# Folding three key blocks into two in a neighbourhood-attention kernel, with a reordered projection piece and exchanged PSUM pools

## The chip, the core and the metric

The kernel runs on one core of a Trainium2 chip. The metric is the device time of one execution in microseconds (us); smaller is better. The engines are named as the profile names them: PE is TensorE's matmul, PEld its weight load, DVE is VectorE, ACT is ScalarE, POOL is GpSimd, and SP is SyncE, which issues most of the DMAs. Each has an instruction queue of its own that runs in order; the engines wait for one another by semaphores.

## The reference

A two-layer encoder trunk on 1024 tokens (a grid of 16 rows by 64 columns) of width 1024, all in float32. Cut to what is computed:

```python
for i in range(2):
    h = rms_norm(x, norm_g[i])
    y = mixer_a(h, ...) if i == 0 else mixer_b(h, ...)
    x = x + y                                  # y already holds the output projection
    g = sigmoid(rms_norm(x, ple_norm_g[i]) @ ple_w_gate[i])
    x = x + g * (p[i] @ ple_w_proj[i])
return rms_norm(x, final_norm_g)

def mixer_a(h):   # 16 heads of 64
    q, k, v, gate = split(h @ w_in, 4)
    # each query sees 8 rows x 16 columns of keys, clamped at the grid's edge, plus a bias by 2-D offset
    o = softmax(q . k[window] / 8 + rpb) @ v[window]
    return (o * silu(gate)) @ w_out

def mixer_b(h):   # 16 query heads, 4 key heads, rms-normalised and rotated q and k, all 1024 keys
    o = softmax(q . k / 8) @ v
    return (o * silu(gate)) @ w_out
```

## The kernel before

**Numbers.** Every float32 operand of a projection is held as a rounded high part and a low remainder, and a product is three matmuls: high by high, high by low, low by high (`split3`). Tile names end in h and l for the two parts (`HTh`/`HTl` the normalised stream, transposed; `wh`/`wl` a weight; `PTh`/`PTl` the transposed softmax numerators).

**Stages.** Mixer A's prologue (norm, first V projection); mixer A's 16 heads; the output projection, gate and norm of layer 0 (`dense_phase(0)`); mixer B's prologue; mixer B; `dense_phase(1)`. The program's order is written out by hand, engine by engine, as the Python code runs; nothing is rescheduled.

**Mixer A.** Tokens are laid out so that a tile of 128 is all 16 rows of an 8-column strip, and there are 8 tiles j. The 16-column window of a query in tile j reaches from its own column in tile j-1 to the column just below it in tile j+1, so an inner tile (j = 1 to 6) needs three key tiles, and an edge tile two. The mask `MK` blocks, in the left tile, columns under the query's and, in the right one, columns at or over it: of each pair of columns in the left and the right tile exactly one is valid. A step is one (head, tile). Its parts:

- `f_S`: two matmuls make the scores `s` of 128 queries against 384 keys (256 at an edge); DVE adds the bias table `tb` and takes the row minimum in one instruction (L741).
- `f_E`: ACT takes the exponential (L750).
- `f_T`: PE transposes each block of 128 into `t` (L758), ACT copies it as `PTh` (L761), DVE writes the remainder `PTl` (L762).
- `f_AV`: two matmuls per key tile, `PTh` and `PTl` by V, add up the output `o`. It runs for the step two back.

`head_end` scales and gates a finished half head. Its two products on POOL, Y by the gate G (L563) and Y by the reciprocal row sums `rb` (L564), are put into the program four steps after the half's last AV, and `rb` comes by two DMAs over DRAM. POOL also makes the bias table (L716, five products a head, at tile 1) and issues the accumulating DMAs that add up weight blocks (L632).

**mix.** In each head a list `att` of these parts is interleaved with a list `dense` of projection pieces (the next head's q and k, the gate, the last embedding product), by weights (`CA` in A, `CB` and `CN` in B): after a part, pieces follow while their share lags. Each part also ticks `post`, a list of callbacks with a delay in parts; `QD` holds the delays of a head's q and k splits. A piece's last matmul calls `leave`, which copies its PSUM bank out. `hold` pieces are kept for the end.

**Mixer B.** A step is one query tile of a head against all 1024 keys: scores in two PSUM banks (`psS`), minimum on DVE (L1198), exponential on ACT (L1204), then eight transposes in two groups of four (L1214), each group copied by ACT (`PTh`, L1216) and DVE (`PTl`, L1217) out of one of two banks `psT`. Two steps share one AV of 16 matmuls, which follows the odd step. `q_stack` (L1168) transposes a new query block into `psT`, once in eight steps. Only one bank `d` serves the projection pieces.

**PSUM.** Eight banks. Pools take banks in the order in which they are opened. `dense_phase` opens `ps_t` (four banks for transposes) and then `ps_d` (four for products); mixer A had opened d, s, t, o with two banks each; mixer B opens d (bank 0), s (1 to 4), t (5 and 6), o (7). Where a stage starts, a bank is free once the last reader of the stage before is through.

## Time and profile before

| | |
|---|---|
| three runs, median (lowest to highest) | 1531.45 us (1528.62 to 1531.79) |
| the profiled execution's own time | 1530.75 us |
| its span, first to last instruction | 1528.9 us (1.85 us lie around it) |
| prologue of A, 0 to 60 us | DVE busy 38.06, ACT 36.11, POOL 15.71 us |
| dense phase of layer 0, 531 to 711 us | PE busy 177.12, DVE 145.11, ACT 79.73 us |
| prologue of B, 711 to 765 us | PE busy 52.94, DVE 43.42 us |
| dense phase of layer 1, 1345 to 1529 us | PE busy 174.08, DVE 139.65 us |

The rows of the two mixers are with the prediction. A row of a view with groups reads: line, engine, operation, output<-inputs, shapes, count | busy us, mean ns of one | idle time of that engine just before them and what ended it. A row of the timeline reads: start, length, engine, line, what, count of merged instructions, and in brackets the engine's idle time before it with its releaser. Matmuls are pipelined, so the length of one overlaps the next; the distance between two starts tells what one costs.

### The profile page before, as it was taken

The page shows a single profiled execution, that of the slowest core. Times are in us where ns is not written, and L with a number is a line of the kernel's source. Part 1 is how long each engine was busy: PE and PEld are TensorE (multiplying, and loading weights), DVE is VectorE, ACT ScalarE, POOL GpSimd, SP SyncE. Part 2 cuts the span into 40 slices and gives each one's busy share as a digit, 9 for nine tenths or more (in the row PEclk, how much of TensorE's full clock was granted, in tenths as well). Part 3 has the DMA queues.
Part 4 walks back from the last instruction along what each step waited for, and adds up shares of the span by engine and source line. Part 5 has one row for each costly group of instructions (what it writes and reads, how often), then busy time and mean ns, then how long its engine had stood idle before and what let it go on. Part 6 is the DMA issues. An engine that isn't in the chain of part 4 may idle for free.

```text
span 1528.9 us, 24361 instructions
## 1 busy us (share of the span) xinstructions
PE 1499.4 (98%) x8976; PEld 1314.0 (86%) x8976; DVE 1102.1 (72%) x2091; ACT 899.4 (59%) x1801; POOL 304.4 (20%) x413
## 2 busy tenths in 40 slices
PE   8999999999999999999999999999999999999997
PEld 8888988988988888888988889989899888878786
DVE  7566576477477599767887786777877877789856
ACT  6565465466366635433467676676767777745432
POOL 1222232142112000010222132453141300000022
PEclk9999999999999999999999999999999999999999
DMA  8325355272122962262210111111101122763123
GB/s 256 119 95 140 83 142 162 63 165 85 36 87 66 334 247 97 90 201 79 77 49 21 32 39 50 46 32 43 58 27 47 37 77 70 234 225 115 67 88 134
DMA packets 91096, 157.22 MB, mean 103 GB/s; under 512 B 18144, under 2 KB 54112, under 8 KB 90464
## 3 DMA queue, kind: packets, MB, share of 16 engines
q1 hardware_dynamic: 85824, 139.66, 27.9%
q0 software_dynamic: 2560, 8.39, 3.2%
q10 hardware_dynamic: 2592, 7.61, 1.4%
q8 instruction: 71, 1.16, 0.3%
q14 instruction: 49, 0.40, 0.1%
HBM read 125.10 MB, written 50.83 MB: 115 GB/s over the span
## 4 chain that ended last, share of the span: by engine, by line
PE 80%; DVE 11%; ACT 5%; issue 2%; DMA 1%; SPq 0%; ACTq 0%; DVEq 0%
PE d L317 50%; PE o L317 10%; PE s L317 8%; PE t L1214 6%; PE t L758 3%; DVE PTl L1217 2%; PE t L317 1%; PE t L467 1%; DVE mn L1198 1%; DVE xn L1541 1%; ACT PTh L1216 1%; ACT P L1204 1%; ACT wh L226 1%; DVE X L1437 1%; DVE HTl L1383 1%
## 5 line engine op out<-in xcount | busy, mean ns | idle before, releaser
L317 PE MATMUL d<-wh,HTh 128*128 128x256 f32 (+1 forms) x1032 | 343.3, 335 | 6.0 <-DVE HTl L469 2.3
L317 PE MATMUL d<-wh,HTl 128*128 128x256 f32 (+1 forms) x1032 | 338.3, 330 | 0.3 <-DVE HTl L469 0.3
L317 PE MATMUL d<-wl,HTh 128*128 128x256 f32 (+1 forms) x1032 | 337.0, 328 | 0.0
L1217 DVE TENSOR_TENSOR PTl<-t,PTh 128x512 fp32r<-128x512 f32 x256 | 164.4, 683 | 111.4 <-ACT PTh L1216 111.1
L317 PEld LDWEIGHTS d<-wh,HTh 128*128 128x128 f32 x1032 | 195.1, 190 | 25.8 <-DVE HTl L469 2.5
L317 PEld LDWEIGHTS d<-wl,HTh 128*128 128x128 f32 x1032 | 194.9, 190 | 19.0
L317 PEld LDWEIGHTS d<-wh,HTl 128*128 128x128 f32 x1032 | 195.1, 190 | 18.7 <-DVE HTl L469 0.5
L317 PE MATMUL d<-HTh,wh 128*128 128x512 f32 x504 | 206.0, 409 | 0.0
L317 PE MATMUL d<-HTh,wl 128*128 128x512 f32 x504 | 198.3, 394 | 0.0
L317 PE MATMUL d<-HTl,wh 128*128 128x512 f32 x504 | 197.6, 392 | 0.0
L1204 ACT ACTIVATE P<-s,mn 128x1024 f32<-128x1024 f32 x128 | 142.8, 1116 | 67.5 <-DVE mn L1198 66.7
L1216 ACT ACTIVATE PTh<-t 128x512 fp32r<-128x512 f32 x256 | 139.7, 593 | 45.1 <-PE t L1214 44.6
L1198 DVE TENSOR_REDUCE mn<-s 128x1 f32<-128x1024 f32 x128 | 154.7, 1209 | 12.3 <-PE s L317 12.3
L1214 PE MATMUL t<-ident,P 128*128 128x128 f32 x1024 | 137.2, 275 | 4.8 <-DVE PTl L1217 1.7
L317 PE MATMUL s<-KA,QS 128*128 128x512 f32 (+2 forms) x384 | 133.7, 402 | 0.0
L1214 PEld LDWEIGHTS t<-ident,P 128*128 128x128 f32 x1024 | 114.7, 140 | 20.1 <-DVE PTl L1217 12.6
L231 DVE TENSOR_TENSOR wl<-wstage,wh 128x1024 fp32r<-128x1024 f32 x78 | 101.7, 1308 | 34.7 <-ACT wh L226 34.2
L317 PE MATMUL s<-KB,QS 128*128 128x512 f32 (+2 forms) x384 | 121.8, 371 | 0.0
L317 PE MATMUL o<-PTh,V 128*128 128x256 f32 (+2 forms) x672 | 118.9, 288 | 1.2 <-DVE Y L483 0.9
L317 PE MATMUL o<-PTl,V 128*128 128x256 f32 (+2 forms) x672 | 119.1, 288 | 0.1
L762 DVE TENSOR_TENSOR PTl<-t,PTh 128x384 fp32r<-128x384 f32 (+1 forms) x128 | 66.6, 520 | 71.3 <-ACT PTh L761 70.1
L317 PEld LDWEIGHTS d<-HTh,wl 128*128 128x128 f32 x504 | 94.7, 188 | 21.6
(237 smaller groups left out, 2700.9 us busy)
## 6 DMA issues: line engine op xcount, KB each, us to landing
wstage<-in_wts SPq DMA_DIRECT2D x88, 512.0 KB
pp<-ppD SPq DMA_DIRECT2D x32, 256.0 KB
X<-in_x SPq DMA_DIRECT2D x15, 512.0 KB
rb<-rD SPq DMA_DIRECT2D x56, 128.0 KB
ppD<-th SPq DMA_DIRECT2D x20, 256.0 KB
tD0t<-in_wts SPq DMA_DIRECT2D x16, 256.0 KB
tD1t<-in_wts SPq DMA_DIRECT2D x16, 256.0 KB
xD<-X SPq DMA_DIRECT2D x8, 512.0 KB
```

The costliest lines, as they stand in the source:

```text
L226: act.activation(hi, s, AF.Copy)
L231: eng.tensor_tensor(lo[:, c:c + n], s[:, c:c + n], hi[:, c:c + n], ALU.subtract)
L317: pe.matmul(ps, a, b, start=first, stop=last, skip_group_check=True)
L467: pe.transpose(ps[:, k], xn[:, (4 * c + k) * 128:(4 * c + k + 1) * 128], ident)
L758: pe.transpose(ps[:, i], sp[:, i * 128:(i + 1) * 128], ident)
L762: dve.tensor_tensor(PTl[:, sl], ps[:, :m], PTh[:, sl], ALU.subtract)
L1198: dve.tensor_reduce(mn, ps, axis=AX.X, op=ALU.min)
L1204: act.activation(p, ps, AF.Exp, bias=mn, scale=-1.0, accum_out=RS[h, hf][:, t:t + 1])
L1214: pe.transpose(ps[:, i], p[:, k * 128:(k + 1) * 128], ident)
L1216: act.activation(PTh[:, ks, c], ps, AF.Copy)
L1217: dve.tensor_tensor(PTl[:, ks, c], ps, PTh[:, ks, c], ALU.subtract)
L1383: dve.tensor_tensor(al(t + m, c), src[m], ah(t + m, c), ALU.subtract)
```

## The change

1. **Folding in mixer A.** For an inner tile, DVE now copies, in PSUM, the right tile's scores over the left tile's wherever the mask `SIDE[:, 2]` (key column under the query's) says so, by `copy_predicated` (128 queries by 128 keys). The left table block gets the right one's entries in the same way, once a head (`join`). Minimum, exponential, transposes and the two copies of the transposed blocks then run on 256 columns, where they ran on 384. POOL takes the folded transposed block apart again: one product by `SIDE[:, :2]` for `PTh` and one for `PTl`, each 128 by 256, into the two places that AV reads. The folded block lies in one of two new slots of `PTh` and `PTl`.
2. AV runs for the step three back, so `head_end` and its POOL products come a step later.
3. The copies of a head's k into the other 64 partitions (`KA`, `KB`) go from DVE to ACT, with five callbacks (`QD` of five) where there were three. A DMA of 192 KB loads `SIDE` in the prologue.
4. **Mixer B.** `mix` puts a projection piece ahead of an odd step's transposes where none has stood since the even step's; `q_stack` waits for the next piece (`after`); three pieces are held for the end where there were two, and the last odd step may take one of them.
5. `dense_phase` opens `ps_d` before `ps_t`: products in banks 0 to 3, transposes in 4 to 7.

```diff
-QD = (2, 5, 8)
+QD = (2, 4, 6, 7, 9)
+    sides = np.stack([c[:, None] >= c[None, :], c[:, None] < c[None, :], c[:, None] > c[None, :]], axis=1).astype(np.float32)
@@ mix
+        since = True
         for i, (f, c) in enumerate(att):
+            kind = getattr(f, "kind", None)
+            if kind == "apart" and not since and (dense or len(kept) > 2):
+                d, e = (dense or kept).pop(0)
+                d()
+                spent += e
+                after.run()
+            if kind in ("apart", "blocks"):
+                since = False
             f()
...
                 spent += c
+                since = True
+                after.run()
@@ qk_evac
-                    def two():
+                    def low_q():
                         dve.scalar_tensor_tensor(qs[hi, s], raw[lo], -0.125, qs[lo, s], op0=ALU.mult, op1=ALU.subtract)
+                    def low_k():
                         dve.tensor_tensor(kb[hi, s], raw[hi], ka[hi, s], ALU.subtract)
-                        dve.tensor_copy(ka[lo, s], ka[hi, s])
-                    def three():
-                        dve.tensor_copy(kb[lo, s], kb[hi, s])
+                    def across(k):
+                        act.activation(k[lo, s], k[hi, s], AF.Copy)
+                    parts = (one, low_q, lambda: across(ka), low_k, lambda: across(kb))
@@
+            def join(h):
+                dve.copy_predicated(TB[h][:, 1], SIDE[:, 2].bitcast(mybir.dt.int32), TB[h][:, 3])
@@ f_S
-                    tb = TB[h][:, 1:4]
-                sp = sb.tile([128, 384], F32, name="sp", bufs=3)
+                    tb = TB[h][:, 1:3]
+                    dve.copy_predicated(ps[:, 0:128], SIDE[:, 2].bitcast(mybir.dt.int32), ps[:, 256:384])
+                sp = sb.tile([128, 256], F32, name="sp", bufs=3)
@@ f_T
-                for i in range(m):
-                    pe.transpose(ps[:, i], sp[:, i * 128:(i + 1) * 128], ident)
+                for i in range(2):
+                    c = 1 - i if inner else i
+                    pe.transpose(ps[:, i], sp[:, c * 128:(c + 1) * 128], ident)
...
+                if inner:
+                    def apart():
+                        for pt in (PTh, PTl):
+                            pool.tensor_tensor(pt[:, 3 * j - 1:3 * j + 4:4], pt[:, f1:f1 + 1].to_broadcast([128, 2, 128]), SIDE[:, :2],
+                                               ALU.mult)
+                    apart()
@@ mixer_a
-                    if n >= 2:
-                        att += av_and_v(*steps[n - 2])
+                    if n >= 3:
+                        att += av_and_v(*steps[n - 3])
@@ mixer_b
-                        att.append((lambda hn=hn, fn=fn: q_stack(hn // 2, fn), 0.0))
+                        att.append((lambda hn=hn, fn=fn: after(lambda: q_stack(hn // 2, fn)), 0.0))
...
-                mix(att, dense, hold=HOLD if g == 3 else 0)
+                mix(att, dense, hold=HOLD + 1 if g == 3 else 0)
@@ dense_phase
+            ps_d = es.enter_context(tc.tile_pool(name="dps", bufs=4, space=PSUM))
             ps_t = es.enter_context(tc.tile_pool(name="dpt", bufs=4, space=PSUM))
-            ps_d = es.enter_context(tc.tile_pool(name="dps", bufs=4, space=PSUM))
```

Three places show how the instructions move. The first is PE in mixer A, at two inner steps of one head: t are the transposes, s the scores, d a projection piece of six matmuls (its first row stands for it), o the AV. Before:

```order
L758 MATMUL t<-ident,sp 128x128 [waits Activation_49]
L758 MATMUL t<-ident,sp 128x128 x2
L317 MATMUL s<-KA,QS 128x384 [waits PE_49]
L317 MATMUL s<-KB,QS 128x384
L317 MATMUL d<-HTh,wh_2073 128x512
...
L317 MATMUL o<-PTh,V 128x384
L317 MATMUL o<-PTl,V 128x384 [waits DVE_49]
```

With the change:

```order
L779 MATMUL t<-ident,sp 128x128 [waits PE_49,Activation_49]
L779 MATMUL t<-ident,sp 128x128
L318 MATMUL s<-KA,QS 128x384 [waits PE_49]
L318 MATMUL s<-KB,QS 128x384
L318 MATMUL d<-HTh,wh_2170 128x512
...
L318 MATMUL o<-PTh,V 128x384 [waits Pool_49]
L318 MATMUL o<-PTl,V 128x384 [waits Pool_49]
```

One transpose of three is gone, the scores stay as they were, and AV now waits for POOL. POOL's own queue over the same stretch of a head gets two products (L789) for every inner step, among the table and the products of `head_end`:

```order
L733 TENSOR_TENSOR tb<-MK,u 128x128 [waits DMAHW6_49]
L733 TENSOR_TENSOR tb<-MK,u 128x128 x4
L789 TENSOR_TENSOR PTh<-PTh,SIDE 128x2x128 [waits Activation_49]
L789 TENSOR_TENSOR PTl<-PTl,SIDE 128x2x128 [waits DVE_49]
...
L577 TENSOR_TENSOR Y<-Y,G 128x512
L578 TENSOR_TENSOR Y<-Y,rb 128x512 [waits DMAHW1_49,DMAHW0_49,Pool_49]
```

The products that wait for the DMA of `rb` stand ahead of later L789 products in the same queue.

The second place is PE at the first two steps of mixer B. Before, the odd step's eight transposes follow the even step's scores directly, and the piece d comes after them:

```order
L1214 MATMUL t<-ident,P 128x128 x8
L317 MATMUL s<-KA,QS 128x512 x2
L317 MATMUL s<-KB,QS 128x512 x2
L1214 MATMUL t<-ident,P 128x128 x8
L317 MATMUL d<-wh_8110,HTh 128x256
```

With the change:

```order
L318 MATMUL s<-KA,QS 128x512 x2
L318 MATMUL s<-KB,QS 128x512 x2
L318 MATMUL d<-wh_8320,HTh 128x256
...
L1247 MATMUL t<-ident,P 128x128 x8
L318 MATMUL s<-KA,QS 128x512 x2
L318 MATMUL s<-KB,QS 128x512 x2
L318 MATMUL o<-PTh,V 128x256 x8
```

The piece has gone ahead of the transposes, and AV (o) now follows the odd step's scores with no piece between.

The third place is PE at the first projection of mixer B's prologue, into bank 0, which follows the last transposes of the dense phase. Before and after:

```order
L467 MATMUL t<-ident,xn 128x128 [waits PE_49,Activation_49]
L467 MATMUL t<-ident,xn 128x128 x3
L317 MATMUL d<-wh_6865,HTh 128x256 [waits DVE_49]
L317 MATMUL d<-wl_6866,HTh 128x256
L317 MATMUL d<-wh_6865,HTl 128x256
```

```order
L481 MATMUL t<-ident,xn 128x128 x3
L318 MATMUL d<-wh_7075,HTh 128x256 [waits Activation_49]
L318 MATMUL d<-wl_7076,HTh 128x256
L318 MATMUL d<-wh_7075,HTl 128x256
```

The wait for DVE, which reads transposes out of their bank, has become one for ACT, which reads products out of theirs.

More of the change, by code (lines that the diff above doesn't have):

```diff
@@ L158, in trunk @@
 @with_exitstack
-def trunk(ctx, tc, x, wts, rpb, gains, hgains, mask, rope, gain0, out):
+def trunk(ctx, tc, x, wts, rpb, gains, hgains, mask, sides, rope, gain0, out):
     nc = tc.nc
@@ L360, in run @@
                 self.left.pop(0)()
-    leave = Evac()
+    leave, after = Evac(), Evac()
+    after.wait = True
     def mix(att, dense, lead=0, hold=0):
@@ L384, in mix @@
                 spent += c
+                since = True
+                after.run()
         leave.run()
+        after.run()
         for f, _ in dense + kept:
@@ L651, in mixer_a @@
             MK = one.tile([128, 5, 128], F32, name="MK")
+            SIDE = one.tile([128, 3, 128], F32, name="SIDE")
             def dalloc():
@@ L933, in mixer_a @@
             f_E(0, 0)
+            join(0)
             f_S(0, 1)
@@ L951, in head @@
                             table(h + 1)
+                        if j == 5 and h + 1 < NH:
+                            join(h + 1)
                         if h >= 1 and j != 1 and jobs:
@@ L969, in mixer_a @@
                 if h == NH - 1:
[L970 removed]
+                    att += [(lambda k=k: f_AV(NH - 1, k), CA[4]) for k in range(NT - 3, NT)]
                 dense = []
@@ L1256, in exps, with blocks, f @@
                 return f
+            def blocks(n):
+                def f():
+                    f_T(*steps[n])
+                f.kind = "apart" if n % 2 else "blocks"
+                return f
             for g in range(4):
```

39 lines of the change are left out of this document (20 added, 19 removed).

## The prediction, made before the change was run

> **What bounds the kernel now.** I read the page first: span, busy shares, and the chain of work that ended last.
>
> ```profile
> span 1528.9 us, 24361 instructions
> ...
> PE 1499.4 (98%) x8976; PEld 1314.0 (86%) x8976; DVE 1102.1 (72%) x2091; ACT 899.4 (59%) x1801; POOL 304.4 (20%) x413
> ...
> PE 80%; DVE 11%; ACT 5%; issue 2%; DMA 1%; SPq 0%; ACTq 0%; DVEq 0%
> ```
>
> PE is hardly ever idle and 80% of the chain is its. So work taken from PE should shorten the span, and work added elsewhere costs only where PE comes to wait for it. The view by stages (columns: window, length, then busy us and count of PE, PEld, DVE, ACT, POOL) says the same of the two mixers:
>
> ```profile
> 60.00:531.00 471.00, 468.50 (x2686) 409.19 (x2685) 300.39 (x666) 277.46 (x620) 106.10 (x130) 1.00 0.42 120
> ...
> 765.00:1345.00 580.00, 570.75 (x3870) 512.02 (x3869) 435.51 (x691) 408.20 (x756) 140.68 (x216) 1.00 0.19 57
> ```
>
> In mixer A POOL has 365 us free, DVE 171, ACT 194, and PE 2.5.
>
> **The transposes of mixer A.** Two rows of the timeline, at an inner and an edge step, and the row of the whole group:
>
> ```profile
> 190.72 0.49 PE L758 MATMUL t<-ident,sp 128*128 128x128 f32 x3
> ...
> 199.47 0.38 PE L758 MATMUL t<-ident,sp 128*128 128x128 f32 x2
> ...
> L758 PE MATMUL t<-ident,sp 128*128 128x128 f32 x352 | 60.2, 275 | 1.4 <-ACT sp L750 1.0
> ```
>
> A third transpose lengthens the run by 0.49 - 0.38 = 0.11 us. Six inner tiles in 16 heads drop one each: 96 x 0.11 = **-10.6 us**. The group's mean of 275 ns would give 26.4, but it holds the pipeline's length, which neighbours share; 0.11 is the value. [...]
>
> The scores stay 384 wide and AV keeps its matmuls, so PE saves nothing else.
>
> **The other engines in mixer A.** Groups of the same stage:
>
> ```profile
> L762 DVE TENSOR_TENSOR PTl<-t,PTh 128x384 fp32r<-128x384 f32 x96 | 53.4, 556 | 62.5 <-ACT PTh L761 61.7
> L741 DVE CUSTOM_DVE_ANT_0 sp<-s,tb 128x384 f32<-128x384 f32 x95 | 52.0, 547 | 10.9 <-PE s L317 10.6
> L694 DVE CAST KB<-KB 64x512 fp32r<-64x512 f32 x30 | 15.1, 504 | 0.9
> L762 DVE TENSOR_TENSOR PTl<-t,PTh 128x256 fp32r<-128x256 f32 x32 | 13.2, 412 | 8.8 <-ACT PTh L761 8.4
> L741 DVE CUSTOM_DVE_ANT_1 sp<-s,tb 128x256 f32<-128x256 f32 x31 | 13.0, 419 | 0.7 <-PE s L317 0.3
> ...
> L761 ACT ACTIVATE PTh<-t 128x384 fp32r<-128x384 f32 x96 | 47.1, 490 | 55.8 <-PE t L758 54.9 <-issue 0.3
> L685 ACT ACTIVATE QS<-th 64x512 fp32r<-64x512 f32 x30 | 18.6, 621 | 0.1
> L761 ACT ACTIVATE PTh<-t 128x256 fp32r<-128x256 f32 x32 | 12.2, 381 | 8.5 <-PE t L758 8.2
> ```
>
> DVE: 128 columns fewer save 0.144 in L762 and 0.128 in L741. The predicated copy is in no row. It moves 128 columns; 412 less the slope of 144 per 128 gives 0.27 us for such an operation, which I take. Below, it can't cost less than the slope alone, 0.14; above, not more than the three-block L762, 0.56. So an inner step gains 0.13 or loses 0.29 on DVE, 96 of them -13 to +28 us, at 0.27 nothing. The two casts per half head leave DVE, some 60 x 0.5 = 30 us, and `join` adds 16 x 0.27 = 4. DVE goes from 300 to about 275 us, off the path. ACT loses 0.11 twice per inner step (21 us) and gains 60 copies of 0.62 (37): 277 becomes 293. The cover of both is their own slack beside PE's 460. If it is gone, transposes wait for the exponential: `across(KB)` stands in ACT's queue two callbacks behind DVE's remainder, so a late DVE holds the exponential and `PTh` behind it.
>
> **POOL in mixer A** gets 192 products of 128 by 256. The nearest rows are POOL's own; the first three are of this stage, the fourth of mixer B, then the longest wait:
>
> ```profile
> L716 POOL TENSOR_TENSOR tb<-MK,u 128x128 f32<-128x128 f32 x70 | 43.1, 770 | 172.0 <-DVE mn L741 168.8 <-DMA u<-U 3.2
> L563 POOL TENSOR_TENSOR Y<-Y,G 128x512 f32<-128x512 f32 x14 | 21.7, 1550 | 54.1 <-DVE Y L483 54.1
> L632 POOL DMA_DIRECT2D tD1t<-tD1t x8 | 8.4, 1424 | 4.4 <-DMA tD1t<-tD1t 4.4
> ...
> L1035 POOL TENSOR_TENSOR qt<-qt,t 128x256 f32<-128x256 f32 x24 | 19.2, 801 | 1.9
> ...
> POOL Y L564 <- DMA rb<-rD: 94.5, 14, 10.8
> ```
>
> The same shape took 0.80 in mixer B; the bounds are the 128-column 0.77 and the 512-column 1.55. At 0.80 POOL's stage load is 106 + 192 x 0.80 = 260 us of 460. A head is tighter: 12 x 0.80, five table products (3.9), and in every second head two Y products for each half (2 x 2.8), 19 us of the shortest heads' 22 or so. It fills only from about 1.05 a product. What stands behind a waiting POOL instruction is new: `rb`'s wait, up to 10.8 us long, was idle time, and now products queue behind it. But it runs while POOL is ahead; in the program it stands a few steps later, and AV uses the products only two steps on, over 5 us. So it is nearly covered.
>
> Contention shows in the trace: while POOL multiplied, DVE's two-input subtraction, 0.80 on average, took 1.79.
>
> ```profile
> L690 DVE TENSOR_TENSOR KB<-th,KA 64x512 fp32r<-64x512 f32 x30 | 24.0, 799 | 0.7
> ...
> 197.82 1.29 POOL L564 TENSOR_TENSOR Y<-Y,rb 128x512 f32<-128x512 f32 x1 [10.78 <-DMA rb<-rD]
> ...
> 197.87 1.79 DVE L690 TENSOR_TENSOR KB<-th,KA 64x512 fp32r<-64x512 f32 x1
> ```
>
> That is 1.0 us, once. Some eight such DVE operations a head meet a POOL that will be busy over half the time, in pieces of 0.8: I estimate 8 x 0.6 x 0.4 = 2 us of DVE per head, within its slack, but a few exponentials will be late. [...]
>
> For new waits in mixer A I put **+3 us**, between 0 (all hidden) and 10 (the transposes' gain given back).
>
> **Mixer B.** The order puts a piece ahead of ten odd transposes that had none. What they waited, and two other kinds of wait (the sixth row is the whole group of `q_stack`, the rest are the timeline's):
>
> ```profile
> 780.19 1.09 PE L1214 MATMUL t<-ident,P 128*128 128x128 f32 x8 [1.16 <-ACT P L1204]
> ...
> 794.59 1.03 PE L1214 MATMUL t<-ident,P 128*128 128x128 f32 x8
> ...
> 795.93 0.63 PE L317 MATMUL s<-KB,QS 128*128 128x512 f32 x2
> 796.60 1.14 PE L1214 MATMUL t<-ident,P 128*128 128x128 f32 x7
> ...
> 865.59 1.19 PE L317 MATMUL o<-PTh,V 128*128 128x256 f32 x8 [0.54 <-DVE Y L483]
> ...
> L1168 PE MATMUL t<-ident,qt 128*128 128x128 f32 x60 | 9.3, 277 | 2.2 <-DVE PTl L1217 2.1
> ...
> 1220.06 0.63 PE L1168 MATMUL t<-ident,qt 128*128 128x128 f32 x4 [0.85 <-DVE PTl L1217]
> ...
> 1339.02 1.25 PE L1214 MATMUL t<-ident,P 128*128 128x128 f32 x8 [1.08 <-DVE PTl L1217]
> ```
>
> The last two scores start at 795.93 and take 0.23 apiece (0.63 for the two less 0.40 for one alone), so the odd transposes could start at 796.39: 0.21 is waiting, and 0.10 more lies between their two groups of four. Measured so, from start to start, the ten waits sum to 5.9 us: first 1.3, last 1.35, one of 0.94, the others 0.3 to 0.4. A piece of 1.4 us (twelve matmuls of 256 columns, or six of 512) covers each. `q_stack`, moved behind a piece, sheds 3.3 (seven waits, 0.15 to 1.0; the group's 2.2 is the part that the pipelined matmul ahead does not hide). Against that, in about ten steps AV now follows the scores bare, as it already did in five: those waited 0.78, 0, 0.38, 0.60 and 0 (the row at 865.59 is the first), mean 0.35, so +3.5. Net **-5.7 us**, between -9.2 (no wait comes back) and +2 (all at 0.78, and only T's 5.9 gained).
>
> **The pools.** Where a stage takes over banks:
>
> ```profile
> 530.72 0.69 DVE L536 TENSOR_TENSOR Y<-Y,t 128x512 f32<-128x512 f32 x1
> ...
> 531.51 0.47 PE L317 MATMUL d<-wh,HTh 128*128 128x512 f32 x1 [1.46 <-ACT G L606]
> ...
> 708.40 0.60 ACT L1598 ACTIVATE th<-d 128x512 f32<-128x512 f32 x1 [2.10 <-PE d L317]
> ...
> 710.37 0.69 DVE L469 TENSOR_TENSOR HTl<-t,HTh 128x512 fp32r<-128x512 f32 x1
> ...
> 711.11 0.39 PE L317 MATMUL d<-wh,HTh 128*128 128x256 f32 x1 [2.31 <-DVE HTl L469]
> ...
> 1346.57 0.60 ACT L606 ACTIVATE th<-d 128x512 f32<-128x512 f32 x1 [1.79 <-PE d L317]
> ```
>
> At 531 PE waits 1.46 us; the row names ACT, but the start falls on the end of DVE's reading of `t` (530.72 + 0.69 = 531.41). With products in bank 0 it waits for the last embedding product's copy instead, about 0.35: **-1.1**. At 711 it waits until 710.37 + 0.69 = 711.06 for the last transposes in bank 0; that becomes the last product's copy, done at 709.00: **-2.1**. At 1346, where nothing waited, the first product now needs bank 0, which holds mixer B's last piece until 1347.17: about **+0.9** (0.6 to 1.2).
>
> The DMA of `SIDE` delays others in the prologue by about a microsecond at most; the first table is needed at 58 us, so I cost it at nothing.
>
> Sum: -10.6 + 3 - 5.7 - 1.1 - 2.1 + 0.9 = -15.6. On the profiled execution's 1530.75 us that is 1515.2; the three runs' median lies 0.7 higher. I say **1515**.
>
> **The rivals.**
> 1. *Mixer B's waits only move*: AV, bare behind the scores, takes what the transposes gave. For it: 865.59. Against: two of five bare AVs waited for nothing. 1515 + 5.7 = 1520.7.
> 2. *DVE and ACT are late in mixer A*: the predicated copy costs near 0.56, `across` holds the exponential. For it: transposes waited for ACT in L758 (1.0 us). Against: both have some 170 us free. 10 instead of 3: 1522, at worst with rival 1 1528.
> 3. *The transposes were hidden*: PE only waits elsewhere. Against: PE's 2.5 us idle in 471. Then the gains in A go, 1515 + 7.6 + rival 1's 5.7 = 1528, no change within noise if another 2 us are late.
> 4. *Slower: POOL becomes the bound of mixer A.* AV waits for L789, `PTh` may not be overwritten before L789 has read, and everything queues. For it: L716's 0.77 for 128 columns against L1035's 0.80 for twice that shows POOL held up in this stage, and L563 took 1.55 where L564 took 1.29. It begins in single heads at 1.05 us a product and decides from (460 - 106) / 192 = 1.84. At 1.95 POOL's stage is 480 us, 20 over PE's: 1535. Against: no group of that shape has a mean over 0.80.
>
> **How the numbers follow.** Forecast 0.55, rival 1 0.13, rival 2 0.13, rival 3 0.04, rival 4 0.15. A measurement of this kernel tells apart about 0.2%, 3 us. Cases one and two and the forecast are faster: 0.81; rival 3 stays within: 0.04; rival 4 is slower: 0.15. The forecast's own range is 1507 to 1521 (its two open terms at their ends). The range goes to 1530 to hold rivals 1 to 3 as well, and leaves out rival 4 and a little below 1507.
>
> **What would show it.** Right: 256 transposes L779 at 0.11 apart; mixer A near 462 us with POOL busy near 260; L789 at 0.75 to 0.9; no PE row waiting for POOL by more than a few us in total; the first product of the dense phase of layer 0 waiting under 0.6, the first of mixer B's prologue starting two microseconds earlier after its transposes, the first of the dense phase of layer 1 waiting near 0.9; odd transposes of mixer B without the waits above. Wrong: L789 over 1.05, PE waiting on POOL or on the exponential for over 10 us, or AV in mixer B waiting for as much as the transposes did.

## The result, and the profile after the change

The change left the time where it was: 1529.74 us (median of 14 runs, 1528.18 to 1534.45) against 1531.22 us (14 runs, 1528.62 to 1531.79) for the kernel before; ratio 0.9999, 95% interval 0.9992 to 1.0006. Each ratio here is taken over all runs of both kernels, with the kernel before timed again in each batch of runs, and so differs a little from the ratio of the two medians. The forecast was 1515.

First the page of the kernel after the change (span, then each engine's busy time), and two rows of its view by stages (window, length, busy us and count of PE, PEld, DVE, ACT, POOL):

```profile
span 1527.8 us, 24694 instructions
...
PE 1489.9 (98%) x8880; PEld 1302.0 (85%) x8880; DVE 1086.6 (71%) x2139; ACT 920.1 (60%) x1865; POOL 448.0 (29%) x605
```

```profile
60.00:531.00 471.00, 458.79 (x2573) 395.85 (x2572) 283.79 (x713) 293.90 (x675) 250.34 (x322) 1.00 0.43 118
...
765.00:1345.00 580.00, 571.18 (x3883) 515.90 (x3881) 438.31 (x695) 409.26 (x759) 141.34 (x217) 1.00 0.19 58
```

PE has lost 9.5 us of busy time and the span 1.1. In mixer A PE's busy time fell from 468.5 to 458.8 us in the same 471, so the time that left PE came back as idle time. DVE, ACT and POOL stand where the prediction put them (275, 293 and 260 us; 284, 294 and 250 here).

Groups of the same stage of the changed kernel (line, engine, operation, output<-inputs, shapes, count | busy us, mean ns | idle before and its releaser):

```profile
L789 POOL TENSOR_TENSOR PTl<-PTl,SIDE 128x256 fp32r<-128x256 f32 x96 | 81.4, 848 | 5.7 <-DVE PTl L785 5.7
L789 POOL TENSOR_TENSOR PTh<-PTh,SIDE 128x256 fp32r<-128x256 f32 x96 | 77.3, 805 | 209.3 <-ACT PTh L784 209.3
L785 DVE TENSOR_TENSOR PTl<-t,PTh 128x256 fp32r<-128x256 f32 x128 | 53.9, 421 | 79.7 <-ACT PTh L784 78.5
L779 PE MATMUL t<-ident,sp 128*128 128x128 f32 x256 | 50.5, 279 | 11.2 <-ACT sp L771 11.2
L763 DVE CUSTOM_DVE_ANT_0 sp<-s,tb 128x256 f32<-128x256 f32 x95 | 40.3, 424 | 3.3
L760 DVE COPY_PREDICATED s<-SIDE,s 128x128 f32<-128x128 int32 x95 | 27.4, 288 | 24.9 <-PE s L318 24.4
L739 DVE COPY_PREDICATED tb<-SIDE,tb 128x128 f32<-128x128 int32 x15 | 10.9, 730 | 0.1
```

The predicated copy takes 0.29 us (0.27 was taken), POOL's products 0.81 and 0.85 (0.80). `join` (L739), the same copy between tables in SBUF, takes 0.73 on average where 0.27 was taken: 0.31 in the two cases in which no POOL instruction ran beside it, 0.45 to 1.26 in the others. The row that differs is L779: the transposes wait 11.2 us for the exponential (L771), before it was 1.0. The view of waits says it more fully (engine, what waited <- for what: us in total, times, longest). Before, for the weight load ahead of the transposes:

```profile
PEld t L758 <- ACT sp L750: 7.0, 20, 1.1
```

After:

```profile
PEld t L779 <- ACT sp L771: 20.7, 27, 2.5
...
ACT Y L533 <- DMA yD0l<-Y: 10.3, 4, 3.8
```

The second line was not there before: ACT waits for a DMA to read the finished output `Y` out of its buffer, so that `head_end` may copy (L533) the next output in. The timeline shows what stands behind it (start, length, engine, what, in brackets the idle time before it):

```profile
197.56 0.50 SPq L570 DMA_DIRECT2D yD0l<-Y  x1
...
203.69 0.59 ACT L533 ACTIVATE Y<-o 64x512 f32<-64x512 f32 x1 [3.81 <-DMA yD0l<-Y]
204.31 0.38 ACT L784 ACTIVATE PTh<-t 128x256 fp32r<-128x256 f32 x1
204.59 0.50 ACT L771 ACTIVATE sp<-sp,mn 128x256 f32<-128x256 f32 x1
...
205.23 0.52 PE L779 MATMUL t<-ident,sp 128*128 128x128 f32 x2 [2.17 <-ACT sp L771]
...
205.98 0.63 PE L318 MATMUL d<-HTl,wh 128*128 128x512 f32 x1
```

The store lands 6 us after its issue; in that time the view by stages gives the core's DMA engines a busy share of 0.91 and more, and 0.41 from 209 to 215 us. The copy stands in ACT's queue ahead of `PTh` and the exponential, and holds both; PE then stands for 2.2 us, and the matmuls after it run at 0.43 us from start to start, where 0.23 is usual, until 209.

To place the rest I use the same stages in every run, from start to start of PE's instructions in the timeline. "A" is mixer A from its first to its last transpose, "A end" from there to the first product of layer 0's dense phase, "dense 0" that phase up to mixer B's first projection, "B" mixer B from first to last transpose, "B end" from there to the first product of layer 1's dense phase. All in us, from the profiled executions; the last column is the median of the timed runs. A profile is one execution: those of tail, qold, dvecopy and best3_13 took 4.1, 2.6, 1.8 and 1.7 us more than their medians, that of fin3 1.8 less, the others are within 0.6:

| kernel | A | A end | dense 0 | B | B end | whole |
|---|---|---|---|---|---|---|
| before | 462.02 | 7.85 | 179.60 | 562.94 | 6.32 | 1530.2 to 1531.2 |
| forecast's steps | -7.6 | -1.1 | -2.1 | -5.7 | +0.9 | 1515 |
| the change | 465.77 | 7.66 | 179.84 | 559.06 | 7.32 | 1529.7 |
| fold | 464.78 | 11.27 | 182.07 | 562.07 | 6.61 | 1538.8 |
| bpart | 462.13 | 7.86 | 179.57 | 559.09 | 6.45 | 1527.5 |
| pools | 462.05 | 7.13 | 177.56 | 561.92 | 7.23 | 1528.0 |
| lag2 | 462.84 | 7.14 | 177.57 | 559.38 | 7.32 | 1526.8 |
| y3 | 459.41 | 7.64 | 179.87 | 559.06 | 7.33 | 1524.7 |
| fin3 | 464.07 | 7.66 | 179.88 | 559.23 | 7.24 | 1531.6 |
| dvecopy | 475.40 | 7.64 | 179.88 | 559.09 | 7.33 | 1539.7 |
| tail | 468.11 | 7.17 | 177.55 | 559.05 | 7.60 | 1528.0 |
| best2 | 459.91 | 7.57 | 177.56 | 559.16 | 6.43 | 1521.5 |
| best3_13 | 470.69 | 7.42 | 177.57 | 559.33 | 6.43 | 1532.0 |
| qold | 473.60 | 7.21 | 177.57 | 559.92 | 6.43 | 1533.7 |
| third | 467.40 | 7.65 | 179.90 | 559.18 | 7.35 | 1532.8 |
| best3_8 | 457.98 | 7.13 | 177.86 | 559.19 | 6.60 | 1520.4 |
| half | 460.10 | 7.65 | 179.88 | 559.10 | 7.32 | 1525.4 |

Mixer B's prologue and the dense phase of layer 1 stay within 0.4 us except in fold (B's prologue +1.3; the mean granted clock of fold's profiled execution is 0.995, that of the change's 0.997). The first score of mixer A starts between 52.3 and 55.0 us in all these profiles, with the same code ahead of it (but for one DMA): differences of 1 to 2 us in the whole are left to that.

In this table the change loses 3.8 us in A although 96 transposes are gone. (The prediction's "near 462" for mixer A does not say from where to where it counts; in this measure its terms give 454.4.) Measured on PE as the distance between starts beyond what the same matmuls take undisturbed (0.11 us for a transpose, 0.23 for 512 columns), PE waits 8.2 us in A before and 22.7 after, 14.6 more; 10.8 us of work are gone. The two sums hang on what is taken as undisturbed, their difference hardly does.

### The profile page after: what moved, and what is told of

Its sections match the earlier page's. It is cut to its first block, busy times and chain, and to the rows that moved or that the text cites. A ratio compares the mean times of both kernels' runs of the same rounds, so it can differ in the third digit from the quotient of the medians.

```text
span 1527.8 us, 24694 instructions
## 1 busy us (share of the span) xinstructions
PE 1489.9 (98%) x8880; PEld 1302.0 (85%) x8880; DVE 1086.6 (71%) x2139; ACT 920.1 (60%) x1865; POOL 448.0 (29%) x605
## 4 chain that ended last, share of the span: by engine, by line
PE 43%; DVE 6%; ACT 2%; issue 1%; POOL 0%; ACTq 0%; DVEq 0%; POOLq 0%
PE d L318 19%; PE o L318 9%; PE s L318 7%; PE t L1247 7%; PE t L318 1%; DVE xn L1580 1%; DVE PTl L1250 1%; DVE X L1476 0%; PE t L1201 0%; DVE wl L232 0%; DVE mn L1231 0%; DVE HTl L483 0%; DVE HTl L1422 0%; ACT PTh L1249 0%; ACT th L1203 0%
## 5 line engine op out<-in xcount | busy, mean ns | idle before, releaser
L1249 ACT ACTIVATE PTh<-t 128x512 fp32r<-128x512 f32 x256 | 139.8, 593 | 53.1 <-PE t L1247 52.3
L1231 DVE TENSOR_REDUCE mn<-s 128x1 f32<-128x1024 f32 x128 | 154.8, 1209 | 11.2 <-PE s L318 10.9
L789 POOL TENSOR_TENSOR PTh<-PTh,SIDE 128x256 fp32r<-128x256 f32 x96 | 77.3, 805 | 209.3 <-ACT PTh L784 209.3
L232 DVE TENSOR_TENSOR wl<-wstage,wh 128x1024 fp32r<-128x1024 f32 x78 | 97.9, 1257 | 32.9 <-ACT wh L227 32.7
```

Of the source, the lines that this page charges most:

```text
L232: eng.tensor_tensor(lo[:, c:c + n], s[:, c:c + n], hi[:, c:c + n], ALU.subtract)
L789: pool.tensor_tensor(pt[:, 3 * j - 1:3 * j + 4:4], pt[:, f1:f1 + 1].to_broadcast([128, 2, 128]), SIDE[:, :2], ALU.mult)
L1231: dve.tensor_reduce(mn, ps, axis=AX.X, op=ALU.min)
L1249: act.activation(PTh[:, ks, c], ps, AF.Copy)
```

## The experiments

**The three parts apart.** fold: parts 1 to 3 of the change, bpart: part 4, pools: part 5, each put alone into the kernel before.

> Parts 1 to 3 alone (the fold, AV three steps back, the copies of k on ACT); mixer B and the pools as before. Theory A (read from the two traces): mixer A as a whole gains nothing, because 10.5 us of transposes are given back as about 14 us of new waits of the remaining transposes for the exponential. Then its stretch from first to last transpose stays near 465.8 us (before: 462.0), and the whole runs at before +2 to +5 us. Rival R (mixer A's 3.8 us come from what the other parts do to it, or from the run, not from the fold): the stretch is near 455 us and the whole 5 to 8 us faster than before.

> Part 4 alone (piece ahead of odd transposes, q_stack later, three held pieces); mixer A and the pools as before. Theory A: the stretch from mixer B's first to last transpose falls from 562.9 to about 559.1 us, and the whole runs 3 to 5 us faster than before. Rival R (the gain in B needs the other parts, or was given back at its end): stretch above 561, the whole within 1.5 us of before.

> Part 5 alone (products in banks 0 to 3 in both dense phases). Theory A: the two waits at the starts go (1.5 us at the first product, 2.3 us ahead of mixer B's prologue), about 2 us of new waits come up inside the dense phase of layer 0, and 0.9 us come up at the start of that of layer 1: sum -0.5 to -1.5, the whole within 2 us of before. Rival R (the new waits inside the dense phase came from mixer A's changed end, not from the pools): none of them here, the whole 2 to 3 us faster.

fold: 1538.79 us, ratio 1.0059 (1.0045 to 1.0073). A is 464.8: the loss in mixer A is the fold's own, as theory A has it. The whole is worse than it said, since the dense phase starts 3.4 us later and is 2.5 us longer:

```profile
529.00:536.00 7.00, 2.87 (x16) 1.94 (x14) 3.89 (x8) 2.63 (x4) 0.00 (x0) 0.91 0.94 365
536.00:541.60 5.60, 5.40 (x13) 4.27 (x14) 4.87 (x7) 2.10 (x3) 0.00 (x0) 0.51 0.20 59
```

In these two rows of fold's view by stages (the number after POOL's is the granted clock) PE stands for about 4 us at the phase's start, and then runs for 5.6 us at a clock of 0.51. What it waits for there was not followed; with the pools exchanged that wait is hardly there. So the parts are not additive: +8.6, -2.6 and -2.1 us by the medians, but -1.5 together.

bpart: 1527.54 us, 0.9986 (0.9977 to 0.9995). B falls by 3.85 us, to the same value as in the whole change: theory A, but the whole gains 2.6 where 3 to 5 were said. What part 4 does does not depend on the others. B itself is 561.9 to 562.9 us in the three profiles that leave it alone (before, fold, pools), so the gain is 2.8 to 3.9.

pools: 1528.01 us, 0.9987 (0.9978 to 0.9995). Here rival R is right: 2.0 us shorter inside the dense phase of layer 0, 0.7 at its start, 0.9 longer at B's end, and no new waits inside. In the whole change those 2.0 us are missing; something in mixer A takes them back (see tail).

**AV two steps back (lag2).** On the whole change:

```diff
-                    if n >= 3:
-                        att += av_and_v(*steps[n - 3])
+                    if n >= 2:
+                        att += av_and_v(*steps[n - 2])
...
```

> The whole change, but AV two steps back again. Theory L (a later head end is what costs in mixer A: its Y buffer comes free late, and its copies fall on those of the next head's q and k): the waits of 6 us for the store of Y and of 3 us at the coincidences go, AV finds POOL's products in time, stretch of mixer A 456 to 460 us, whole 5 to 9 us under the change. Theory P (AV needs the third step because POOL's products come late): AV waits for POOL in every head where the table or the Y products stand ahead, stretch above 468 us, whole slower than the change.

1526.76 us, 0.9975 (0.9966 to 0.9984). Neither theory alone. Its waits:

```profile
PEld o L318 <- POOL PTl L789: 8.2, 10, 1.2
PEld t L779 <- ACT sp L771: 7.2, 19, 1.4
```

The transposes wait no more than before the change (7.2 against 7.0), and ACT's wait for `yD0l` is gone: L is right that the later head end causes that one. How much of the transposes' other waits goes with it this run cannot tell, since PE now stands elsewhere. But AV now waits for POOL's products, 11.0 us of PE by the distances, where it is 1.5 in the change. The third step buys the one and pays with the other.

**A third Y buffer (y3).** On the whole change: `name="Y", bufs=2` becomes `bufs=2 if layer else 3`.

> The whole change with a third Y buffer in mixer A. Theory Y (ACT's copy of the output into Y stands ahead of PTh and the exponential, and waits for the store of the Y two pairs back): the four waits of ACT for that DMA (10.3 us in the profile of the change) go, and with them the transposes' waits at 205, 256 and 329 us, 4.5 us, and 1.6 us of slower matmuls behind the first: stretch of mixer A 459 to 461 us (change: 465.8), whole 5 to 7 us under the change. Rival (something else is late at these places as well): ACT's DMA wait gone, transposes still waiting there, stretch above 463.

1524.65 us, 0.9957 (0.9945 to 0.9969). A is 459.41, 6.4 under the change (5.1 by the medians of the whole): theory Y. ACT's wait for the DMA is not in the view any more, the transposes' is down to

```profile
PEld t L779 <- ACT sp L771: 15.2, 23, 1.4
```

and PE's longest wait for the exponential is 1.1 us, where it is 2.2 in the change. A buffer of 2 KB per partition takes back 6.4 of the 14.6 us of new waits.

**The head end's products a step earlier (fin3).** On the whole change: `FIN = (4, 4)` becomes `(3, 4)`.

> The whole change, with head_end's products three steps after the half's last AV instead of four, that is at the place in the program where they stood before the change. Theory L (the later head end is the cause): the Y buffer is stored a step earlier, so the waits for it (6 us with the slow matmuls) go or fall under 1 us, and the copy of the finished half no longer falls on the splits of the next q and k (six waits of 0.5 us): stretch of mixer A 456 to 459 us. Rival K (the copies of k on ACT are the cause of the 0.5 us waits): those waits stay, stretch 459 to 461.

1531.64 us, 1.0006 (0.9996 to 1.0016). A 464.07, both theories too low. The waits for `Y` are gone, but others took their place:

```profile
POOL Y L578 <- DMA rb<-rD: 30.3, 10, 4.5
PEld o L318 <- POOL PTh L789: 3.7, 3, 1.6
```

POOL comes to the product by `rb` before the DMA has brought it (that wait is 3.1 us in the change), and holds the products of the fold behind it; AV waits for them. Here is the wait that the prediction feared for POOL; the later head end of the change is what keeps it small.

**The copies of k back on DVE (dvecopy).** On the whole change:

```diff
-QD = (2, 4, 6, 7, 9)
+QD = (2, 5, 8)
...
-                    parts = (one, low_q, lambda: across(ka), low_k, lambda: across(kb))
+                    def two():
+                        low_q()
+                        dve.tensor_tensor(kb[hi, s], raw[hi], ka[hi, s], ALU.subtract)
+                        dve.tensor_copy(ka[lo, s], ka[hi, s])
+                    def three():
+                        dve.tensor_copy(kb[lo, s], kb[hi, s])
+                    parts = (one, two, three)
```

> The whole change, but the copies of k to the other partitions back on DVE, with the old delays. Theory K (the 60 copies on ACT make the exponential late): the waits at 62 to 75 us and those of 0.64 us once in four heads go, 3 to 5 us, waits for Y stay: stretch of mixer A 461 to 463 us. Rival D (DVE with 30 us more is late instead): the minimum comes late, PE waits at other places, stretch 465 to 472 us.

1539.71 us, 1.0058 (1.0045 to 1.0071). Rival D, and stronger than it said: A is 475.4. DVE's groups in mixer A of this kernel:

```profile
L708 DVE TENSOR_TENSOR KB<-th,KA 64x512 fp32r<-64x512 f32 x30 | 37.9, 1264 | 0.5
L709 DVE CAST KA<-KA 64x512 fp32r<-64x512 f32 x30 | 27.6, 921 | 0.7
...
L712 DVE CAST KB<-KB 64x512 fp32r<-64x512 f32 x30 | 16.0, 533 | 0.9
```

and the cast of `KA` before the change:

```profile
L691 DVE CAST KA<-KA 64x512 fp32r<-64x512 f32 x30 | 14.1, 469 | 0.9
```

Beside a POOL with 192 more products the subtraction goes from 0.80 to 1.26 us and this cast from 0.47 to 0.92, 28 us in all; the cast of `KB` goes from 0.50 to 0.53 only, and the minimum and the remainder of `PTl` stay at 0.42. On ACT the same copies take 0.63 each. So part 3 is, on balance, what lets the fold run beside POOL. ACT's wait for `yD0l` is nearly gone in this execution (0.7 us), so the fair comparison for A is y3's 459.4: 16 us. Theory K is right in one point: the pairs of waits once in four heads are gone here, so part 3 has a share in them (below). The run moves the delays (`QD`) together with the copies and does not separate the two.

**AV two steps back in the last head alone (tail).** On the whole change, from the last head's third step on, `steps[n - 2]` is taken in place of `steps[n - 3]`.

> The whole change, with AV two steps back in the last head only (from its third step). Theory E (what part 5 gains at the dense phase of layer 0 is lost there because mixer A ends a step later, with its last products and its DMAs behind): last transpose to dense phase 7.1 instead of 7.7 us, dense phase of layer 0 177.6 instead of 179.8 us as in the run with the pools alone, mixer A's last head 1 to 2 us shorter: whole 3 to 5 us under the change. Rival (the losses inside the dense phase are chance): 179 us or more again, whole within 1.5 us of the change.

1528.03 us, 0.9985 (0.9976 to 0.9993). Dense phase 177.55 and start 7.17: theory E. This is where the 2 us of the pools went. The whole is 1.7 us under the change, where 3 to 5 were said. A itself is longer, 468.1: the profiled execution, 1532.11 us, is the slowest of the twelve, ACT waited longer for the store of `Y` in it, and the third Y buffer was not there:

```profile
ACT Y L533 <- DMA yD0l<-Y: 13.7, 5, 4.0
```

**Together (best2).** y3 and tail on the whole change, and the exchanged banks in layer 0 only:

```diff
-            ps_d = es.enter_context(tc.tile_pool(name="dps", bufs=4, space=PSUM))
-            ps_t = es.enter_context(tc.tile_pool(name="dpt", bufs=4, space=PSUM))
+            first, second = ("dps", "dpt") if l == 0 else ("dpt", "dps")
+            pools = {n: es.enter_context(tc.tile_pool(name=n, bufs=4, space=PSUM)) for n in (first, second)}
+            ps_d, ps_t = pools["dps"], pools["dpt"]
```

> The change with a third Y buffer in mixer A, AV two steps back in the last head only, and the products' banks first in layer 0's dense phase alone (layer 1 as before the change). If the effects are additive, against the run with the third Y buffer (1524.7): dense phase of layer 0 -2.3, its start -0.5, mixer A's last head about -1, start of layer 1's dense phase -0.9: 1519 to 1521 us. Rival (they share a cause, and one takes the other's place): 1523 or more.

1521.50 us, 0.9941 (0.9928 to 0.9953). Dense 0 -2.3 and B's end -0.9 against y3 as expected; the last head brought nothing in A, and the start of the dense phase 0.1 instead of 0.5, so that the whole ends 0.5 above the range said.

**What is left in mixer A.** In y3 PE's waits above 0.09 us lie in four places: 2.5 us in the first head, 1.9 in the last, six waits of 0.5 where the copy of a finished half (L574) lies in ACT's queue ahead of the splits of the next q and k, and three pairs of 0.64 and 0.45, one in four heads, where the projection of V ends. One such pair, in the timeline of the change:

```profile
184.96 0.63 ACT L710 ACTIVATE KA<-KA 64x512 fp32r<-64x512 f32 x1
185.62 1.06 ACT L227 ACTIVATE wh<-wstage 128x1024 fp32r<-128x1024 f32 x1
...
186.85 0.50 ACT L771 ACTIVATE sp<-sp,mn 128x256 f32<-128x256 f32 x1
...
187.39 1.44 DVE L232 TENSOR_TENSOR wl<-wstage,wh 128x1024 fp32r<-128x1024 f32 x1
...
187.49 0.44 PE L779 MATMUL t<-ident,sp 128*128 128x128 f32 x2 [0.47 <-ACT sp L771]
...
187.72 1.72 POOL L789 TENSOR_TENSOR PTl<-PTl,SIDE 128x256 fp32r<-128x256 f32 x1
...
189.65 0.51 ACT L771 ACTIVATE sp<-sp,mn 128x256 f32<-128x256 f32 x1 [1.24 <-DVE mn L763]
...
190.31 0.44 PE L779 MATMUL t<-ident,sp 128*128 128x128 f32 x2 [0.30 <-ACT sp L771]
```

For the first wait, ACT has its copy of `KA` (`across`, part 3) and a weight's high part in the queue ahead of `PTh` and the exponential; before the change PE waited 0.3 here. For the second, the exponential waits for DVE's minimum, which stands behind a weight's remainder (L232) that takes 1.44 beside a POOL product of 1.72, where the means are 1.26 and 0.85.

best3_13 and best3_8 move L574 in best2 (`YS = (11, 11)` becomes `(13, 11)` and `(8, 11)`); half and third are on y3.

> The same, with the copy of a finished half (L574 on ACT) two parts later, behind the exponential instead of ahead of the splits of the next q and k. Theory S (six waits of 0.5 us come from these copies lying together on ACT): these waits go, mixer A 2 to 3.5 us under that of the kernel above. Rival: the copy makes the next exponential late instead, mixer A within 1 us.

1531.98 us, 1.0017 (1.0003 to 1.0031): A 10.8 us longer, the opposite of theory S. The timeline of one of the six places:

```profile
123.64 0.61 ACT L574 ACTIVATE rb<-Y 128x512 fp32r<-128x512 f32 x1
...
124.29 0.88 DVE L575 TENSOR_TENSOR Y<-Y,rb 128x512 fp32r<-128x512 f32 x1 [0.65 <-ACT rb L574]
125.20 1.66 DVE L704 SCALAR_TENSOR_TENSOR QS<-th,QS 64x512 fp32r<-64x512 f32 x1
126.89 0.42 DVE L763 CUSTOM_DVE_ANT_1 sp<-s,tb 128x256 f32<-128x256 f32 x1
127.36 0.51 ACT L771 ACTIVATE sp<-sp,mn 128x256 f32<-128x256 f32 x1 [2.18 <-DVE mn L763]
128.01 0.44 PE L779 MATMUL t<-ident,sp 128*128 128x128 f32 x2 [1.77 <-ACT sp L771]
```

ACT is no longer the one that is late; DVE is, because its remainder of the half (L575) now waits for ACT and stands ahead of the minimum, with the next subtraction (L704), which takes 1.66 here instead of 0.79, beside POOL's product by the gate (L577, 1.74 us from 124.57 us on). Six waits of 0.5 became six of 2.0 us, and the mean granted clock of the profiled execution is 0.995, where it is 0.998 in best2.

> The fastest kernel so far (third Y buffer, AV two steps back in the last head, products' banks first in layer 0 alone; mixer A 459.9 us), with the copy of a finished half on ACT (L574) three parts earlier, behind an exponential and ahead of the copy of the piece (L697). Theory S (the six waits of 0.5 us at 123, 195, 244, 316, 364 and 436 us come from L574 ahead of the splits): they go or fall below 0.2, mixer A 457 to 458 us, whole 1518.5 to 1520. Rival (ACT has the same sum of work between two exponentials wherever L574 lies there, or waits for POOL's product): mixer A 459.5 or more.

1520.38 us, 0.9933 (0.992 to 0.9945), the fastest of all. A is 1.9 us shorter than in best2. Of the six waits two fell, to 0.29 us, and four stayed at 0.5: L574 still lies between the same two exponentials there, only ahead of other copies, and the rival's sum of work holds. Why two fell was not followed. The rest of the 1.9 us is one wait of AV, 0.6, and the last head.

> The kernel with the third Y buffer (mixer A 459.4 us); from the second head on POOL multiplies only the first 64 of the 128 columns of each block, so the other half of the unfolded blocks keeps the first head's values. POOL's products fall from 0.84 to about 0.45 us, its load from 262 to about 190 us. Theory C (POOL's products hold up DVE, and the exponential with it): the waits of 0.46 us once in four heads go and the others shrink, mixer A 457 us or less. Rival N (POOL is off the path): the same waits at the same places, mixer A 458.7 to 460.

```diff
+                        w = 128 if h == 0 else 64
                         for pt in (PTh, PTl):
-                            pool.tensor_tensor(pt[:, 3 * j - 1:3 * j + 4:4], pt[:, f1:f1 + 1].to_broadcast([128, 2, 128]), SIDE[:, :2],
+                            pool.tensor_tensor(pt[:, 3 * j - 1:3 * j + 4:4, :w], pt[:, f1:f1 + 1, :w].to_broadcast([128, 2, w]), SIDE[:, :2, :w],
```

1525.43 us, 0.9964 (0.995 to 0.9977). POOL's groups in mixer A, products of half the width:

```profile
L790 POOL TENSOR_TENSOR PTl<-PTl,SIDE 128x128 fp32r<-128x128 f32 x90 | 53.7, 596 | 15.3 <-DVE PTl L785 11.3
L790 POOL TENSOR_TENSOR PTh<-PTh,SIDE 128x128 fp32r<-128x128 f32 x90 | 45.9, 510 | 230.9 <-ACT PTh L784 230.6
```

The products fell to 0.51 and 0.60 us, not to 0.45. A is 460.10, no shorter. The three waits of 0.45 are halved, 0.7 us in all, the last head waits 1.3 more, the others are the same: rival N but for the three, in which DVE's remainder runs beside POOL's product (1.44 us in the pair above, 1.26 on average). With AV three steps back POOL is otherwise off the path, and what is left is the order and sum of ACT's and DVE's queues.

**Transposes put back (third).** On y3, `pe.transpose(ps[:, 2], sp[:, :128], ident)` once more at each inner step.

> The kernel with the third Y buffer (mixer A 459.4 us), with a third transpose put back at each inner step; nothing reads its result. Theory F (a transpose costs 0.11 us on PE, and the waits for the exponential stand elsewhere): 96 x 0.11 = 10.6, less what the ten transposes that wait would absorb, mixer A 467 to 470 us. Rival H (the third transpose ran in time in which PE waits anyway): mixer A 459 to 463 us.

1532.79 us, 1.0012 (1.0004 to 1.0021): A +8.0 us, theory F. By the distances between starts the extra transposes take 10.5 us and shorten the other waits by 2.5. The price of 0.11 was right, and three quarters of it are on the path.

**The place of q_stack (qold).** On best3_13, `q_stack` directly instead of through `after`.

> The same as the kernel with the later copy, but q_stack in mixer B at its old place, with no wait for the next piece. Theory Q (q_stack behind a piece only moves its wait: 2.9 us less of its own, but 0.4 to 0.7 us more in seven steps for the second group of transposes, which finds its bank taken by q_stack): mixer B within 1 us of 559.1. Rival (its move is a gain): mixer B 2 to 3.5 us longer.

1533.70 us, 1.0019 (1.0008 to 1.0031), B 559.92 against 559.33: theory Q. By the distances `q_stack` waits 3.6 instead of 0.9 us, and the second groups of transposes 3.8 instead of 7.2; AV behind the scores waits 2.4 more. The timeline of the change shows one of these exchanges:

```profile
1087.24 0.60 PE L1201 MATMUL t<-ident,qt 128*128 128x128 f32 x4
...
1087.67 0.60 PE L1247 MATMUL t<-ident,P 128*128 128x128 f32 x4
1087.87 0.60 ACT L1203 ACTIVATE th<-t 128x512 f32<-128x512 f32 x1 [0.69 <-PE t L1201]
...
1088.53 0.66 PE L1247 MATMUL t<-ident,P 128*128 128x128 f32 x4 [0.25 <-ACT th L1203]
```

There are two banks `psT`. `q_stack` takes one directly ahead of a step's transposes, whose second group must wait until ACT has emptied it.

## Why the prediction was wrong, point by point

The measured 1529.7 lies at the upper end of the range, which was drawn up to 1530 for rivals 1 to 3; that is luck, since rivals 1 and 3 are not how it came about, and rival 2 only in part. The forecast's own range is also mis-summed: its two open terms at their ends give 1508.5 to 1529.7, not 1507 to 1521.

**The transposes, -10.6.** Right in size: 10.8 us of PE's work are gone, and third gives 8.0 us of stage time for the same 96. Rival 3 (they were hidden) falls: by third no more than a quarter of them was.

**New waits in mixer A, +3 between 0 and 10.** This is the step that failed: they are 14.6 us. PE's row for the transposes alone waits 11.2 us for the exponential, the prediction's own sign of being wrong. The costs of the single operations on DVE, ACT and POOL were right to a few hundredths but for `join` (0.73 instead of 0.27), and the three sums per stage to 10 us. What failed is the sentence that called their slack beside PE's 460 us the cover. The transposes wait for one ACT instruction per step, and that came late where something ahead of it in ACT's queue came late (by 3.81 us at 203.69 us), though ACT was busy for only 294 us of the 471.
- 6.4 us came from a wait that no term and no rival named: I followed AV's third step to POOL's products (rightly: lag2 pays 9.5 us without it), but not through `head_end` to the store of `Y`, the reuse of its buffer and the copy in ACT's queue. That costs 4.5 us of waits and 1.6 of slowed matmuls; y3 shows it.
- About 8 us are the short waits listed above, from ACT's and DVE's order. Rival 2 had this kind of wait, at 10 us. Of its two causes one is wrong: the predicated copy costs 0.29, not 0.56. The other, that `across` holds the exponential, is seen ahead of the first wait of each pair behind the V projections (0.64 us, 0.3 before the change), while in sum the copies of k on ACT save 10 us or more (dvecopy). That these waits hang on the order of ACT's queue is shown where L574 was moved (two of six shrank, and six grew with the other place); that the second waits of the pairs hang on POOL's products is shown by half. For the first waits of the pairs dvecopy bears it out without separating it from the delays; for those in the first and the last head the cause is only read from the timeline.

**DVE's contention with POOL, 2 us a head.** Smaller in the change, and elsewhere: `join` takes 0.42 us more than without a POOL instruction beside it, once a head, the subtraction of k went from 0.80 to 0.87 us on average, and the remainders of the weights fell from 1.39 to 1.26. In sum that is well under 1 us a head, but it stands ahead of the exponential in the pairs of waits. dvecopy shows where more would have been: 28 us in the stage, had the casts stayed on DVE.

**POOL, and rival 4.** Right: products at 0.81 and 0.85, no PE row that waits for POOL in the change's view of waits, and half shows that less POOL work gains 0.7 us of waits and no time.

**Mixer B, -5.7.** It gave -3.9, by bpart and the whole change alike (2.8 to 3.9 with B's own variation). The mechanism was right, two of its sizes were not. The waits of the odd transposes that got a piece ahead went from 5.9 to 1.2 us, -4.7; what is left is one at step 103, which rose from 0.4 to 1.2. `q_stack`'s own wait fell by 2.7 to 0.6 (3.3 forecast). AV bare behind the scores cost 1.0 instead of 3.5: at the stage's beginning it waits for nothing. Not in the sum were 3.0 us at other transposes, most of them for the bank that `q_stack` now takes; its move is worth 0.6 us by qold, less than B varies by. These items sum to -3.4; the other 0.5 was not followed.

**The pools, -1.1, -2.1, +0.9.** Alone they gave -0.7, -2.0 and +0.9. In the whole change the two waits at the starts went as forecast:

```profile
533.17 0.50 PE L318 MATMUL d<-wh,HTh 128*128 128x512 f32 x1 [0.30 <-ACT G L620]
...
713.01 0.39 PE L318 MATMUL d<-wh,HTh 128*128 128x256 f32 x1 [0.25 <-ACT th L1637]
...
1345.23 0.50 PE L318 MATMUL d<-wh,HTh 128*128 128x512 f32 x1 [0.74 <-ACT th L620]
```

(1.46, 2.31 and nothing before). But mixer A ends a step later with AV three steps back; its end gave 0.9 us of the first back, and 2.1 us of new waits, mostly for DVE, inside the dense phase took the second, one of them

```profile
594.57 0.47 PE L318 MATMUL d<-wh,HTh 128*128 128x512 f32 x1 [0.56 <-DVE X L1476]
```

tail brings the second back, and half of the first. How a later end of A reaches DVE 60 us on was not followed further. The DMA of `SIDE`, put at nothing, leaves no mark: the first score starts at 53.2 to 54.6 us in the three profiles without it, at 52.3 to 55.0 with it.

Summed: 11.4 us of the missing 14.5 are mixer A's, 2.3 the dense phase's, 1.8 mixer B's, 0.9 mixer A's end; 1.9 came as an earlier start of mixer A in the profiled execution, which is no effect of the change.

## What to carry to other kernels

Where one instruction per step releases the bottleneck, the slack of its engine over a stage says nothing of its cover (ACT here: 294 us busy of 471, and PE waited 11.2 us for it): go through that engine's queue and ask of every instruction ahead of it what it may wait for, buffers that a DMA must first empty included. When a step is moved later, follow its outputs to the end, to the last store and the next user of each buffer, since the largest single loss here stood two heads behind the edit and took one small buffer to mend. And measure the parts of a change apart: that showed which two side effects to mend, and the mended change takes 0.9933 of the time before.

## What the runs showed of the chip that I had not expected

In the change, after PE had stood for 2.2 us, matmuls of 512 columns ran at 0.43 us from start to start instead of 0.23. The view by stages of the changed kernel for the stretch behind that wait, at 205 us:

```profile
205.20:209.00 3.80, 3.77 (x12) 3.20 (x13) 1.53 (x6) 0.98 (x3) 3.07 (x6) 0.55 0.78 170
```

The granted clock is 0.55 there, and 1.00 ahead of it (202.00 to 205.20 us) and behind it (209.00 to 215.00). The clock's record in the same trace has 0.50 for 3.41 us, from 205.45 to 208.86, and 1.00 from there to 1523. In fold, where PE stood for about 4 us, the two rows shown with that run give, as an estimate, 6.7 us at half the clock (7.00 x 0.09 x 2 + 5.60 x 0.49 x 2). A wait as long did not always come with it: in the kernel before PE's starts lie 2.58 us apart at 711 us, against 2.51 at 205 us in the change, and the granted clock from 711 to 718 us is 1.00. What decides between the two was not shown. In the change the slow stretch cost 1.6 us on top of a wait of 2.2.
